# The chunked heads' part of the output projection, by column halves and earlier

## The chip, the cores and the metric

The kernel runs on one core of a Trainium2 chip. The metric is the device time of one execution in microseconds; the time before is the median of three runs. All details come from one profiled execution.

## The reference, cut to what matters

One layer of a streaming encoder, 1024 tokens, 1024 channels, float32. The projection at issue is `mixed`, whose input is the concatenation of two groups of eight heads:

```
q   = rmsnorm(q_lat) @ w_q_up      # latent heads: low-rank q and kv,
kv  = rmsnorm(kv_lat) @ w_kv_up    # "up" projections, rope, QK norm
o_mla = mla_attention(q, k, v)               # 8 heads x 64
o_ca  = chunk_attention(cq, ck, cv, bias)    # 8 heads x 64
mixed = concat([o_mla, o_ca]) @ w_out        # (1024 x 1024) @ (1024 x 1024)
x = x + g_a * mixed
x = x + g_m * gated_conv_mlp(norm(x))
```

Rows 512 to 1023 of `w_out` belong to the chunked heads. Their product needs nothing of the latent heads, so it can be formed while these are still running; the kernel does so and adds the latent heads' share later.

## The kernel before, in words

Every float32 product is made of three matmuls on halves of the numbers: a value is split into a rounded part (`hi_of`, L75, on ScalarE here) and the rest (`lo_of`, L83, mostly on GpSimd), and high x high, high x low and low x high are summed in PSUM (`gemm3`, L150 on; the matmuls are L154, L155 and L156).

The attention runs as 32 units (L974): 16 of the chunked heads and then 16 of the latent heads, each one head and one half of the tokens, with four query tiles of 128 rows. Of each tile `scores` (L735) makes the scores on PE, their minimum on VectorE (L783), the exponential on ScalarE (L790), the scaled probabilities and their rest on GpSimd (L73) and VectorE (L812), and transposes them by a DMA on SyncE's queue (L824). `values` (L829), three tiles later, multiplies by the values on PE (L852), and at the end of a unit the result goes through ScalarE and VectorE (L861, L862) to DRAM, `oT_d`.

All else is given to the attention as filler: `fillers` (L924) is a list of generators in a fixed order, which end with `m` (latent projection), `up0` and `up1` (up projection of latent heads 0 to 3 and 4 to 7, `f_up`, L591) and `oca` (the chunked heads' output projection, `f_oca`, L669). A generator yields the cost in ns of each group of matmuls that it has emitted. `pace` (L961) lets fillers emit as much cost as the attention's own cost times a ratio, `R_CA` = 1.9 in the chunked heads and `R_MLA` = 0.5 in the latent heads (L47). `need` (L952) emits fillers until a named one is done: the first latent unit needs `up0`, the second needs `up1` (L920). Filler groups are tied behind an attention instruction a few steps back (`trail`, L161).

What is emitted is then put in an order for each engine at compile time by a planner that simulates the engines: it takes the ready instruction with the lowest number, where the attention's scores, probabilities and values count as emitted 400, 200 and 200 instructions earlier (L42). On the chip each engine runs its own list in order.

`f_up` emits for each of 8 token tiles nine matmuls (`qu`, `ku`), copies and squares on ScalarE, and norms, rotary and rest on VectorE. `f_oca` loads and splits eight weight tiles (`load_wo`, L657, 128 x 512 each, two column halves), and then for each of 8 token tiles loads 128 x 512 of `oT_d` (`cl`), splits it (`ch`, `cl`), and makes both column halves: 12 matmuls each into a PSUM tile of tag `mm` (two buffers, shared with `f_up`), a copy on ScalarE (`co`, tag `sq`, two buffers) and a store to `part_d`.

Buffers: tag `R` (four) holds the raw rows of `f_up` and `cl`, `ch`; tag `A` (five) holds raw weights; tag `G4` (eight) holds the six split weights of the up projections and then the eight of `f_oca`. After the attention `load_wo(0, n)` (L997) loads the latent heads' eight weight tiles into `G4` again, `o_load` (L1007) the latent results, and the output projection `op` runs on PE.

Of the kernel before, what the change touches and what calls it, by code (L numbers as in the profile page):

```python
# [13 lines left out]
F32 = mybir.dt.float32  # L14
F32R = mybir.dt.float32r
# [49 lines left out]
def layer_kernel(ctx, tc, I, out):  # L65
# [70 lines left out]
    def rtile(name, shape=(P, 512), dt=F32):  # L136
        return apg.tile(list(shape), dt, name=name, tag="R", bufs=4)

    def qtile(name):
        return apg.tile([P, 512], F32, name=name, tag="sq", bufs=2)  # L140
# [450 lines left out]
    def f_up(gr):  # L591
        if gr == 0:
            right.__exit__(None, None, None)
            for i in "4v3":
                G["cm" + i] = tc.tile_pool(name="gp" + i, bufs=1, side="right", reuse_waits="tile")
                G[i] = G["cm" + i].__enter__()
        wq = []
        for k in range(2):
            raw = qtile(f"wqr{gr}_{k}")
            sp.dma_start(raw[:, :384], I["w_qu"][gr][:, k, :])  # L600
            w = g4([P, 2, 512], F32R, f"wq{gr}_{k}")
            hi_of("a", w[:, 0, :384], raw[:, :384])
            lo_of("p", w[:, 1, :384], raw[:, :384], w[:, 0, :384])
            wq.append(w)
        raw = qtile(f"wkr{gr}")
        sp.dma_start(raw[:], I["w_kvu"][gr])
        ssw = cst.tile([P, 1], F32, name=f"sswm{gr}")
        junk = qtile(f"wkj{gr}")
        act.activation(junk[:, 0:256].rearrange("p (a b) -> p a b", a=4),
                       raw[:].rearrange("p (a b) -> p a b", a=4)[:, :, NOPE:], AF.Square, accum_out=ssw[:])  # L610
        vscale["m", gr] = pow2_scale(f"m{gr}", ssw[:], gb2[:], 1, float(KVR))
        sc = vscale["m", gr][0]
        wk = g4([P, 2, 512], F32R, f"wk{gr}")
        hi_of("a", wk[:, 0], raw[:])
        lo_of("p", wk[:, 1], raw[:], wk[:, 0])
        for t in range(NT):
            h, j = divmod(t, 4)
            sl = slice(j * P, (j + 1) * P)
            if t % 2 == 0:
                mq[gr, t // 2] = g3([P, 2, 4, QK], F32, f"qn{gr}_{t}")  # L620
                mk[gr, t // 2] = g3([P, 2, 4, QK], F32, f"kn{gr}_{t}")
                mv[gr, t // 2] = G["v"].tile([P, 2, 4, 2, 64], F16, name=f"vt{gr}_{t}", tag="Gv", bufs=8)
            pt = ps.tile([P, 512], F32, name=f"qu{gr}_{t}", tag="mm", bufs=2)
            yield from gemm3_f(pt[:, :384], [(latT[k, h][:, 0, sl], latT[k, h][:, 1, sl], wq[k][:, 0, :384], wq[k][:, 1, :384])
                                for k in range(2)])
            rq = rtile(f"uqr{gr}_{t}")
            act.activation(rq[:, :384], pt[:, :384], AF.Copy)
            sq = qtile(f"usq{gr}_{t}")
            act.activation(sq[:, :384], rq[:, :384], AF.Square)
            ss = cst.tile([P, 8], F32, name=f"uss{gr}_{t}", tag="ss", bufs=4)  # L630
            r = cst.tile([P, 8], F32, name=f"ur{gr}_{t}", tag="rr", bufs=4)
            dve.tensor_reduce(ss[:, 0:4], sq[:, :384].rearrange("p (a b) -> p a b", a=4), axis=AX.X, op=ADD)
            pt = ps.tile([P, 512], F32, name=f"ku{gr}_{t}", tag="mm", bufs=2)
            yield from gemm3_f(pt[:], [(latT[2, h][:, 0, sl], latT[2, h][:, 1, sl], wk[:, 0], wk[:, 1])])
            p4 = pt[:].rearrange("p (a b) -> p a b", a=4)
            raw = rtile(f"kraw{gr}_{t}")
            r3 = raw[:, :256].rearrange("p (a b) -> p a b", a=4)
            act.activation(r3, p4[:, :, 0:NOPE], AF.Copy)
            s3 = raw[:, 256:512].rearrange("p (a b) -> p a b", a=4)
            act.activation(s3, r3, AF.Square)  # L640
            dve.tensor_reduce(ss[:, 4:8], s3, axis=AX.X, op=ADD)
            dve.tensor_tensor(ss[:, 4:8], ss[:, 4:8], ssr[:, t:t + 1].to_broadcast([P, 4]), op=ADD)
            rsqrt_mean(r[:], ss[:], QK)
            v_t = mv[gr, t // 2][:, t % 2]
            act.activation(v_t[:, :, 0, :], p4[:, :, NOPE:], AF.Copy, scale=sc)
            dve.scalar_tensor_tensor(v_t[:, :, 1, :], p4[:, :, NOPE:], sc, v_t[:, :, 0, :], op0=MUL, op1=SUB)
            q_t = mq[gr, t // 2][:, t % 2]
            dve.tensor_tensor(q_t, rq[:, :384].rearrange("p (a b) -> p a b", a=4),
                              r[:, 0:4].unsqueeze(2).to_broadcast([P, 4, QK]), op=MUL)
            rope_apply(q_t[:, :, NOPE:], q_t[:, :, NOPE:], tabq, t, 4, rq[:, 0:256], dve)  # L650
            k_t = mk[gr, t // 2][:, t % 2]
            dve.tensor_tensor(k_t[:, :, 0:NOPE], r3, r[:, 4:8].unsqueeze(2).to_broadcast([P, 4, NOPE]), op=MUL)
            dve.tensor_tensor(k_t[:, :, NOPE:], kr[:, t:t + 1, :].to_broadcast([P, 4, ROPE]),
                              r[:, 4:8].unsqueeze(2).to_broadcast([P, 4, ROPE]), op=MUL)


    def load_wo(k0, n, he, le):  # L657
        ws = []
        for k in range(k0, k0 + 4):
            raw = atile(f"wor{k}_{n}")  # L660
            sl = slice(n * 512, (n + 1) * 512)
            sp.dma_start(raw[:], I["w_out"][k * P:(k + 1) * P, sl])
            w = g4([P, 2, 512], F32R, f"wo{k}_{n}")
            hi_of(he, w[:, 0], raw[:])
            lo_of(le, w[:, 1], raw[:], w[:, 0])
            ws.append(w)
        return ws

    def f_oca():  # L669
        ws = [load_wo(4, n, "a", "p") for n in range(2)]  # L670
        for t in range(NT):
            lo = rtile(f"cl{t}", (P, 4, P), F32R)
            hi = rtile(f"ch{t}", (P, 4, P), F32R)
            sp.dma_start(f32(lo[:]), oT_d[4:8, :, t * P:(t + 1) * P].rearrange("k p t -> p k t"))
            hi_of("a", hi[:], f32(lo[:]))
            lo_of("p", lo[:], f32(lo[:]), hi[:])
            for n in range(2):
                pt = ps.tile([P, 512], F32, name=f"oc{t}_{n}", tag="mm", bufs=2)
                yield from gemm3_f(pt[:], [(hi[:, k], lo[:, k], ws[n][k][:, 0], ws[n][k][:, 1]) for k in range(4)])
                o = qtile(f"co{t}_{n}")  # L680
                act.activation(o[:], pt[:], AF.Copy)
                sp.dma_start(part_d[t][:, n * 512:(n + 1) * 512], o[:])


    def q2(name):
# [222 lines left out]
    def mla_unit(gr, hh, g):  # L908
        o = hh % 2

        def prep():
# [10 lines left out]
        return u  # L922

    fillers = [("v0", f_v(0)), ("qk1", f_qk(1)), ("qk2", f_qk(2)), ("v1", f_v(1)), ("qk3", f_qk(3)),  # L924
               ("m", f_m()), ("up0", f_up(0)), ("up1", f_up(1)), ("oca", f_oca())]
    done = set()
    side = [f_ada()]
    nside = [0]
# [1 line left out]
    def fill_step():  # L930
        while fillers:
            key, gen = fillers[0]
            try:
                c = next(gen)
            except StopIteration:
                done.add(key)
                fillers.pop(0)
                continue
            if key == "qk1":
                if rope[0] is None:  # L940
                    rope[0] = rope_tables()
                with tc.issue_after(anchor["dve"]):
                    next(rope[0], None)
            if key not in ("v0", "up0", "up1", "oca"):
                nside[0] += c
                while nside[0] > 1700:
                    nside[0] -= 1700
                    next(side[0], None)
            return c
        return None  # L950
# [10 lines left out]
    def pace(cost, ratio):  # L961
        debt[0] += cost * ratio
        while debt[0] > 0:
            c = fill_step()
            if c is None:
                debt[0] = 0.0
                return
            debt[0] -= c

    with tc.issue_after(anchor["pe"]):  # L970
        for _ in range(NPRE):
            fill_step()
# [4 lines left out]
    for n in range(len(tiles) + DEPTH):  # L977
        if n < len(tiles):
            u, i = tiles[n]
            if i % 4 == 0:  # L980
                need(u.need)
                u.prep()
            pace(u.scores(i), R_CA if u.band else R_MLA)
        if n >= DEPTH:
            u, i = tiles[n - DEPTH]
            if i % 4 == 1:
                need(u.needv)
            if i % 2:
                pace(u.values(i), R_CA if u.band else R_MLA)
    need(["oca"])  # L990
    for _ in side[0]:
        pass
# [591 lines left out]
```

## Time and profile before

| What | Value |
|---|---|
| Median of 3 runs (lowest, highest) | 1364.86 us (1364.09, 1369.03) |
| The profiled execution, its span | 1366.2 us, 1364.4 us |
| TensorE clock granted, mean | 0.943 |

Where the time lies, from the profile's table of stretches (busy us of each engine):

| Stretch, us | What runs | PE | DVE | ACT | POOL | Clock |
|---|---|---|---|---|---|---|
| 0 to 98 | norm, modulation, first projection | 68.21 | 72.39 | 43.37 | 52.75 | 0.93 |
| 98 to 393 | chunked heads, projections as filler | 260.44 | 216.69 | 134.56 | 161.85 | 0.90 |
| 393 to 420 | first up projection | 17.95 | 24.18 | 15.81 | 14.29 | 0.92 |
| 420 to 440 | first latent tiles, second up projection begins | 14.78 | 17.22 | 10.57 | 15.90 | 0.60 |
| 640 to 690 | end of attention, output projection | 41.73 | 28.14 | 16.88 | 25.90 | 0.85 |
| 690 to 1364 | gated MLP | 656.89 | 571.21 | 295.96 | 201.03 | 0.99 |

The stretches between 440 and 640, which the change touches, are shown in the prediction. PE is the matmul part of TensorE, PEld its weight loads, DVE is VectorE, ACT ScalarE, POOL GpSimd, SP SyncE, which issues the DMAs. A matmul's busy time overlaps the next one's start, so a busy PE is not one at its peak.

### The profile page before, as it was taken

To read this page: it belongs to the slowest core of one execution; us is meant where nothing else is said; L and a number is where in the kernel's file an instruction comes from. 1 tells how busy PE (TensorE), PEld (TensorE's weight loads), DVE (VectorE), ACT (ScalarE), POOL (GpSimd) and SP (SyncE) were. 2 spreads that over 40 slices of the span, in tenths; PEclk is the share of its full clock that TensorE was granted. 3 is DMA by queue.
4 is the path that set the end of the run, shared out by engine and by line. 5 is a ranking of instruction groups with operands and counts; after the bars stand their busy time and mean duration, and the time that the engine had idled before them with its cause. 6 is when DMAs were issued, how large, how long until landed. Compare 5 with 4: busy or idle time off the path is not lost.

```text
span 1364.4 us, 18704 instructions
## 1 busy us (share of the span) xinstructions
PE 1224.4 (90%) x6168; PEld 1007.3 (74%) x6168; DVE 1103.3 (81%) x1928; ACT 620.9 (46%) x1131; POOL 571.1 (42%) x610
## 2 busy tenths in 40 slices
PE   4889798999877779887898999999999998999998
PEld 3878586877655657665677888888888886888886
DVE  6957879576578997887689888889999997687667
ACT  4443445344455645453357544443344344434331
POOL 5453557376546484334652544443444432000000
PEclk9899797999886879997998999999999999999999
DMA  8413658657222368667940333333333335963441
GB/s 318 136 34 80 144 146 186 166 124 162 62 55 77 72 136 176 143 136 159 374 179 31 112 105 128 104 116 101 131 108 131 104 113 203 369 198 115 125 163 61
DMA packets 223689, 190.57 MB, mean 140 GB/s; under 512 B 148708, under 2 KB 166884, under 8 KB 223592
## 3 DMA queue, kind: packets, MB, share of 16 engines
q1 hardware_dynamic: 223592, 189.38, 48.4%
q8 instruction: 48, 0.79, 0.2%
q14 instruction: 49, 0.40, 0.1%
HBM read 117.24 MB, written 37.49 MB: 113 GB/s over the span
## 4 chain that ended last, share of the span: by engine, by line
PE 31%; DVE 14%; issue 5%; ACT 3%; DMA 3%; POOL 1%; SPq 0%; DVEq 0%; ACTq 0%; POOLq 0%
PE p L1068 4%; PE p L1070 4%; PE p L1069 4%; DVE u L1238 3%; DVE u L1237 2%; PE dnA_P L1395 2%; PE dnA_P L1397 2%; PE dnA_P L1396 2%; PE dnB_P L1395 1%; PE dnB_P L1397 1%; PE dnB_P L1396 1%; ACT u L1236 1%; DVE we L84 1%; DMA PTm<-hlm 1%; DVE ws L1087 1%
## 5 line engine op out<-in xcount | busy, mean ns | idle before, releaser
L77 ACT ACTIVATE dnP<-dnr 128x1024 fp32r<-128x1024 f32 x73 | 77.3, 1062 | 116.4 <-PE dnA_P L1397 46.4
L1369 DVE TENSOR_TENSOR dnP<-dnr,dnP 128x1024 fp32r<-128x1024 f32 x72 | 88.5, 1232 | 51.1 <-ACT dnP L77 51.1
L73 POOL TENSOR_SCALAR hlm<-Pm,rim 128x512 f16<-128x512 f32 (+3 forms) x96 | 67.5, 711 | 76.4 <-ACT Pm L790 21.6
L1237 DVE SCALAR_TENSOR_TENSOR u<-c,cvp,u 128x1023 f32<-128x1023 f32 x44 | 67.1, 1566 | 27.8 <-ACT u L1236 27.8
L84 POOL TENSOR_TENSOR wf<-wu,wf 128x512 fp32r<-128x512 f32 x22 | 38.7, 1757 | 117.6 <-ACT wf L77 117.6
L73 POOL TENSOR_SCALAR hlc<-Pc,ric 128x640 f16<-128x640 f32 (+2 forms) x64 | 47.2, 741 | 71.0 <-DVE ric L793 45.9
L812 DVE SCALAR_TENSOR_TENSOR hlm<-Pm,rim,hlm 128x512 f16<-128x512 f32 (+3 forms) x96 | 67.9, 715 | 9.1 <-POOL hlm L73 8.6
L790 ACT ACTIVATE Pm<-sm,mm 128x128 f32<-128x128 f32 (+3 forms) x64 | 47.2, 738 | 52.7 <-DVE mm L783 32.0
L1236 ACT ACTIVATE u<-c,cvp 128x1024 f32<-128x1024 f32 x44 | 52.3, 1237 | 29.1 <-DVE c L1329 19.1
L852 PE MATMUL pvm<-PTm,vt 128*128 128x256 f16 (+1 forms) x320 | 46.0, 296 | 20.8 <-DMA PTm<-hlm 14.2
L790 ACT ACTIVATE Pc<-sc,mc 128x640 f32<-128x640 f32 (+2 forms) x64 | 42.0, 658 | 48.7 <-DVE mc L779 36.6
L1238 DVE SCALAR_TENSOR_TENSOR u<-c,cvp,u 128x1022 f32<-128x1022 f32 x44 | 63.8, 1488 | 0.0
L812 DVE SCALAR_TENSOR_TENSOR hlc<-Pc,ric,hlc 128x640 f16<-128x640 f32 (+2 forms) x64 | 53.2, 837 | 11.7 <-POOL hlc L73 11.5
L84 POOL TENSOR_TENSOR wb<-wu,wb 128x512 fp32r<-128x512 f32 x22 | 36.4, 1655 | 56.5 <-ACT wb L77 49.5
L852 PEld LDWEIGHTS <-vt 128*128 128x128 f16 x320 | 31.9, 109 | 35.6 <-issue 14.6
L155 PE MATMUL ipq<-wq_s,hT 128*128 128x256 f32 x192 | 55.9, 292 | 0.5 <-POOL wq_s L84 0.5
L154 PE MATMUL ipq<-wq_s,hT 128*128 128x256 f32 x192 | 55.3, 290 | 0.7 <-ACT wq_s L77 0.7
L156 PE MATMUL ipq<-wq_s,hT 128*128 128x256 f32 x192 | 55.4, 289 | 0.0
L77 ACT ACTIVATE wc<-ws 128x512 fp32r<-128x512 f32 x21 | 13.3, 632 | 84.3 <-DVE ws L1087 65.0
L1397 PE MATMUL dnA_P<-dnP 128*128 128x512 f32 x132 | 51.4, 389 | 0.0
L1396 PE MATMUL dnA_P<-dnP 128*128 128x512 f32 x132 | 51.4, 389 | 0.0
L1395 PE MATMUL dnA_P<-dnP 128*128 128x512 f32 x132 | 51.2, 389 | 0.0
(432 smaller groups left out, 4442.3 us busy)
## 6 DMA issues: line engine op xcount, KB each, us to landing
wu<-w_up SPq DMA_DIRECT2D x44, 512.0 KB, 3.5
dnr<-g_d SPq DMA_DIRECT2D x73, 256.0 KB, 2.8
aw<-w_ada SPq DMA_DIRECT2D x48, 256.0 KB, 3.5
g_d<-u SPq DMA_DIRECT2D x22, 512.0 KB, 3.1
dnr<-w_down SPq DMA_DIRECT2D x44, 256.0 KB, 5.4
adaw<-w_ada_a SPq DMA_DIRECT2D x16, 512.0 KB, 5.5
x<-x SPq DMA_DIRECT2D x16, 512.0 KB, 8.8
g_d<-gs SPq DMA_DIRECT2D x22, 256.0 KB, 2.7
```

The source lines that it names most:

```text
L73: pool.tensor_scalar(o, i, s, 1.0, op0=MUL, op1=MUL)
L77: act.activation(o, i, AF.Copy)
L84: (pool if eng == "p" else dve).tensor_tensor(o, i, f32(hi), op=SUB)
L790: act.activation(pr[:, :n], sv, AF.Exp, bias=m[:], scale=-1.0, accum_out=rsum[:, 0:1])
L812: dve.scalar_tensor_tensor(hl[:, w:2 * w], pp, ri[:], hl[:, :w], op0=MUL, op1=SUB)
L852: last = pe.matmul(dst, u.vst(j), mov, start=(x == 0), stop=(x == len(todo) - 1), skip_group_check=True)
L1237: dve.scalar_tensor_tensor(u[:, 1:], c[:, :S - 1], cvp[:, cv + 1:cv + 2], u[:, 1:], op0=MUL, op1=ADD)
L1238: dve.scalar_tensor_tensor(u[:, 2:], c[:, :S - 2], cvp[:, cv:cv + 1], u[:, 2:], op0=MUL, op1=ADD)
L1369: r = f(*a, **k)
L1395: pe.matmul(pt, sh, w[:, 0, 0], start=start, stop=False, skip_group_check=add)
L1396: pe.matmul(pt, sh, w[:, 1, 0], start=False, stop=False, skip_group_check=add)
L1397: pe.matmul(pt, sl, w[:, 0, 0], start=False, stop=stop, skip_group_check=add)
```

## The change

`f_oca` makes one column half for a call, with its own four weight tiles, and loads and splits the eight `oT_d` tiles for that half. A new filler `mix` takes the place of `up1`: it alternates one token tile of the second up projection with one token tile of the first column half. The half's tiles come from tag `A`; `up1` counts as done when its eighth tile is emitted. The filler `oca` then makes the second column half, with tiles of tag `R`, and from the end of `mix` on the pace in the latent heads is 0.6 x 0.5.

```
     def f_up(gr):
         ...
                               r[:, 4:8].unsqueeze(2).to_broadcast([P, 4, ROPE]), op=MUL)
+            yield None

-    def f_oca():
-        ws = [load_wo(4, n, "a", "p") for n in range(2)]
+    def f_oca(n, buf):
+        ws = load_wo(4, n, "a", "p")
         for t in range(NT):
-            lo = rtile(f"cl{t}", (P, 4, P), F32R)
-            hi = rtile(f"ch{t}", (P, 4, P), F32R)
+            lo, hi = (buf(f"c{x}{t}_{n}") for x in "lh")
             sp.dma_start(f32(lo[:]), oT_d[4:8, :, t * P:(t + 1) * P].rearrange("k p t -> p k t"))
             hi_of("a", hi[:], f32(lo[:]))
             lo_of("p", lo[:], f32(lo[:]), hi[:])
-            for n in range(2):
-                pt = ps.tile([P, 512], F32, name=f"oc{t}_{n}", tag="mm", bufs=2)
-                yield from gemm3_f(pt[:], [(hi[:, k], lo[:, k], ws[n][k][:, 0], ws[n][k][:, 1]) for k in range(4)])
-                o = qtile(f"co{t}_{n}")
-                act.activation(o[:], pt[:], AF.Copy)
-                sp.dma_start(part_d[t][:, n * 512:(n + 1) * 512], o[:])
+            pt = ps.tile([P, 512], F32, name=f"oc{t}_{n}", tag="mm", bufs=2)
+            yield from gemm3_f(pt[:], [(hi[:, k], lo[:, k], ws[k][:, 0], ws[k][:, 1]) for k in range(4)])
+            o = qtile(f"co{t}_{n}")
+            act.activation(o[:], pt[:], AF.Copy)
+            sp.dma_start(part_d[t][:, n * 512:(n + 1) * 512], o[:])
+            yield None
+
+    def f_mix():
+        up, oc = f_up(1), f_oca(0, lambda nm: apg.tile([P, 4, P], F32R, name=nm, tag="A", bufs=5))
+        for t in range(NT):
+            for c in up:
+                if c is None:
+                    break
+                yield c
+            if t == NT - 1:
+                done.add("up1")
+            for c in oc:
+                if c is None:
+                    break
+                yield c

-               ("m", f_m()), ("up0", f_up(0)), ("up1", f_up(1)), ("oca", f_oca())]
+               ("m", f_m()), ("up0", f_up(0)), ("mix", f_mix()),
+               ("oca", f_oca(1, lambda nm: rtile(nm, (P, 4, P), F32R)))]

+            if c is None:
+                continue
-            if key not in ("v0", "up0", "up1", "oca"):
+            if key not in ("v0", "up0", "mix", "oca"):

+    def rate(u):
+        return R_CA if u.band else 0.6 * R_MLA if "mix" in done else R_MLA

-            pace(u.scores(i), R_CA if u.band else R_MLA)
+            pace(u.scores(i), rate(u))
-                pace(u.values(i), R_CA if u.band else R_MLA)
+                pace(u.values(i), rate(u))
```

## The prediction

> **What bounds the kernel now.** I read the page first, then busy time by stage, then the stretch that the change touches.
>
> ```profile
> span 1364.4 us, 18704 instructions
> ...
> PE 1224.4 (90%) x6168; PEld 1007.3 (74%) x6168; DVE 1103.3 (81%) x1928; ACT 620.9 (46%) x1131; POOL 571.1 (42%) x610
> ```
>
> The table of stretches has, for each engine, busy us and instructions, then the granted TensorE clock, the DMA share and GB/s:
>
> ```profile
> 440.00:500.00 60.00, 42.27 (x216) 32.82 (x217) 57.18 (x170) 34.29 (x80) 37.89 (x39) 0.83 0.46 96
> 500.00:640.00 140.00, 122.16 (x692) 96.96 (x691) 116.31 (x284) 69.45 (x144) 61.47 (x82) 0.95 0.73 150
> ```
>
> From 440 to 500 us the second up projection runs beside the first latent heads. DVE is the bound: 57.18 of 60 us (95%), while PE is idle for 60 - 42.27 = 17.7 us. From 500 to 640 the rest of the latent attention runs beside the whole chunked-head projection; there PE (87%) and DVE (83%) hinder each other in turn. Where the projection's matmuls (`oc`) lie, and how many softmax tiles pass (one L783 reduction each), is seen in the same table for one tile and for one line:
>
> ```profile
> 500.00:520.00 20.00, 13.51 (x50) 8.90 (x50) 0.00 (x0) 2.37 (x4) 1.00 0.82 155
> 600.00:620.00 20.00, 6.18 (x24) 4.30 (x24) 0.00 (x0) 1.03 (x2) 1.00 0.70 132
> ...
> 480.00:500.00 20.00, 3.11 (x5) 0.66 0.62 138
> 500.00:520.00 20.00, 4.77 (x6) 1.00 0.82 155
> 600.00:620.00 20.00, 5.51 (x9) 1.00 0.70 132
> ```
>
> With 50 projection matmuls in 20 us, 6 tiles pass; with 24 of them, 9 pass; none lies before 500. So the filler is dense where it hurts, and absent where PE waits. The chain of waits over 500 to 640, shares of that window by line, then three of its steps:
>
> ```profile
> by line: DMA PTm<-hlm 8.3%; PE sm L764 7.5%; issue 5.5%; PE pvm L852 5.1%; ACT Pm L790 2.5%; PE oc L154 2.3%; PE oc L155 2.1%; PE oc L156 2.1%; DVE hlm L812 2.0%; ACT om L861 1.5%; POOL hlm L73 1.3%; ACT mk L704 1.0%; DVE mm L783 0.7%; PE m
> ...
> 579.36 0.02 issue
> ...
> 609.66 0.24 PE oc L156
> 609.90 0.23 PE oc L154
> 610.13 0.23 PE oc L155
> ```
>
> The projection holds 2.3 + 2.1 + 2.1 = 6.5% of 140 us, 9.1 us, and all of it behind 579.36, where this chain enters the window. One such matmul costs 0.23 us on the chain (its own duration, about 0.40, overlaps the next).
>
> **The change, part by part.** Instructions that it doubles or moves:
>
> ```profile
> L154 PE MATMUL oc<-wo,ch x64: 392/398/628, 500.7 to 629.9; 128*128 128x512 f32 x64
> ...
> L674 SPq DMA_DIRECT2D cl<-oT_d x8: 377/409/574, 494.3 to 590.4; - x8
> L77 ACT ACTIVATE ch<-cl x8: 622/632/634, 497.6 to 593.5; 128x512 fp32r<-128x512 f32 x8
> L84 POOL TENSOR_TENSOR cl<-cl,ch x8: 1272/1280/1708, 499.6 to 594.2; 128x512 fp32r<-128x512 f32 x8
> ...
> DMA to landing us min/median/max: 3.0/3.2/3.9
> ```
>
> *Matmuls.* Three lines of 64, 192 in all; unchanged. Half, 96 x 0.23 = 22 us of PE time, moves into the stretch of the second up projection.
>
> *Gain in 500 to 640.* By the chain: 9.1 us in the 60.6 us from 579.36 to 640, halved, is 4.55; over 140 us that is 140 / 60.6 x 4.55 = 10.5 us. By the other bound: no DVE work leaves, so 116.31 us at the 95% reached before 500 gives 122 us, a gain of 18 at most. Below, zero: other chains (the transposes' landing) may stand right behind. I take 11, next to the chain row. The later rate, 0.6 x 0.5 = 0.3 of attention cost, spreads the other 96 thinner; by the planner's formulas the remaining attention (L827 and L867 summed: 10.1 us a head, eight heads less the first unit, 78 us) pays for 23 us of filler, and 20.7 are left (96 at 215.8 ns, L172), so the second half should end shortly before the attention does.
>
> *Cost in 440 to 500.* 22 us of matmuls meet 17.7 us of idle PE, so at best 4.4 us stick out. Beside it stands the new split work. Each half now loads and splits its own 8 tiles: 8 more of each row above, 8 x 1.28 = 10.2 us POOL, 8 x 0.63 = 5 us ACT, 8 x 0.41 = 3.3 us on SP's queue and 8 x 256 KB. ACT has 25.7 us idle in the stretch, which hides its part; DMA is 46% busy, which hides the loads if they are issued early. POOL's part touches DVE:
>
> ```profile
> 427.20 2.62 POOL L84 TENSOR_TENSOR wo<-wor,wo 128x512 fp32r<-128x512 f32 x2
> ...
> 427.52 1.17 DVE L462 TENSOR_TENSOR qn<-uqr 128x64 f32<-128x64 f32 x1
> 428.61 1.30 DVE L463 TENSOR_TENSOR qn<-uqr 128x64 f32<-128x64 f32 x1
> ...
> 497.22 0.20 DVE L462 TENSOR_TENSOR qn<-uqr 128x64 f32<-128x64 f32 x1
> 497.34 0.21 DVE L463 TENSOR_TENSOR qn<-uqr 128x64 f32<-128x64 f32 x1
> ```
>
> The same two rotary operations take 0.2 us undisturbed, and 1.17 and 1.30 while POOL runs two splits: about 1 us lost for each. Eight splits enter the stretch, and three weight splits of the other half should leave it:
>
> ```profile
> 477.18 1.35 POOL L84 TENSOR_TENSOR wo<-wor,wo 128x512 fp32r<-128x512 f32 x1
> ...
> 480.11 1.29 POOL L84 TENSOR_TENSOR wo<-wor,wo 128x512 fp32r<-128x512 f32 x1
> ...
> 485.08 1.61 POOL L84 TENSOR_TENSOR wo<-wor,wo 128x512 fp32r<-128x512 f32 x1 [0.92 <-ACT wo L77]
> ```
>
> Net five, 5 us of an engine that is 95% busy. The 4.4 and the 5 lie beside each other, so I take 5, with 0 and 22 (no idle gap usable) as ends. The Trainium skill ("SBUF — State Buffer", section "SBUF: two separate sides") calls the port pair of DVE and GpSimd an exclusive lock: an operation that finds it held waits for the whole instruction. The two rows agree; by that rule alone all eight splits could cost their full 1.28 us, 10 instead of 5, and the net gain would shrink to 3.
>
> *New waits.* In PE's in-order queue the matmuls of each projection tile wait for its load, its ACT copy and its POOL split; scores, values and page transposes queue behind, and DVE waits for those. In SP's queue the load of a tile two ahead waits for a buffer (5 in its pool, two per tile); the probability transposes queue behind it, and the value matmuls wait for them. On ACT the copy out of PSUM waits for PE, with exponentials behind it. All are hidden if the planner's order fits the chip; the price if not is a rival below. The result's copy shares two buffers with the up projection's squares; a buffer is held until its store has landed, a few us against some 7.5 us per up-projection tile (60 us / 8). I cost it at nothing.
>
> *The end.* The last weights (`wo`, second use) now find four of their eight buffers free early:
>
> ```profile
> 642.92 1.54 SPq L662 DMA_DIRECT2D wor<-w_out x3
> 643.54 3.38 PE L852 MATMUL pvm<-PTm,vt 128*128 128x256 f16 x16 [2.77 <-DMA PTm<-hlm]
> ...
> 647.93 0.63 ACT L77 ACTIVATE wo<-wor 128x512 fp32r<-128x512 f32 x1 [1.35 <-DMA wor<-w_out]
> 648.58 0.68 ACT L861 ACTIVATE om<-pvm,vabm 64x512 f32<-64x512 f32 x1
> ...
> 651.21 0.79 PE L154 MATMUL op<-wo,oh 128*128 128x512 f32 x1 [4.29 <-ACT oh L77]
> ```
>
> The last values end at 643.54 + 3.38 = 646.92, but their copy starts only at 648.58, behind a weight copy that waited for its load: 1.7 us. The output projection waits 4.3 us for `oh`, queued behind the same copies. So 1.7 to 4.3 us; I take 2, next to the first, since the next stage hangs on that copy's store.
>
> **Sum:** -11 + 5 - 2 = -8 us. The profiled execution took 1366.2 us (span 1364.4 and 1.8 around it), so 1358.2; it stood 1.3 above the median 1364.86, so 1357 by the median. A measurement here can tell about 0.5%, 6.8 us, so the line lies at 1358.
>
> **Rivals.**
>
> *The gain is taken by the next chain (same).* Landing transposes (8.3%) and issue (5.5%) outweigh the projection's 6.5%. If only 4 of the 11 us remain, -4 + 5 - 2 = -1: 1364. For it: DVE at 83% already. Against: the 9 tiles of 600 to 620.
>
> *POOL is late and PE stands in its queue (slower).* POOL in 480 to 500:
>
> ```profile
> 480.00:490.00 10.00, 4.96 (x21) 3.49 (x20) 9.88 (x25) 6.95 (x17) 8.67 (x10) 0.69 0.39 97
> 490.00:500.00 10.00, 6.64 (x30) 5.16 (x31) 9.97 (x33) 3.73 (x10) 9.74 (x9) 0.62 0.84 180
> ```
>
> POOL is 87 and 97% busy there. A projection tile whose split comes late holds the attention behind it. If all eight tiles wait as long as the L852 row above did for its transposes (2.77 us), 22 us come on top: -11 + 5 - 2 + 22 = +14, 1379. It decides once the wait passes (8 + 6.8) / 8 = 1.9 us per tile. For it: this stretch. Against: in 440 to 480 POOL is much freer.
>
> *Both engines fill up (much faster).* DVE's bound, -18; the up stretch not longer; the end -4: -22, 1343. It needs the granted clock, 0.62 and 0.69 in those rows, to come up as the gaps fill. The Trainium skill ("TensorE: Matmul & The Clock Gate", section "Part 1: The HAM clock gate") says that an idle window of some 3.4 us halves the clock and a busy one restores it. By that rule, steady filler is worth up to 0.17 x 42 = 7 us of PE time in the stretch, an estimate; the rows agree as far as low clocks stand beside idle PE.
>
> *The planner leaves the first half behind the up projection (the change does not do what it says).* Then only the doubled splits stay, 0 to +8, say 1367. Against: in program order each projection tile stands ahead of the next up-projection tile.
>
> **How the numbers follow.** Forecast 0.42 (1350 to 1358); next chain 0.26; POOL late 0.18 (of it, a small part below +14); much faster 0.10; unchanged place 0.04. Faster by over 0.5%: 0.42 + 0.10 = 0.52. Within: 0.26 + 0.04 = 0.30. Slower: 0.18. The range runs from 1344, about the DVE bound, to 1371, where the slower case begins: it leaves out the slower case, and little below.
>
> **What would show it.** Projection matmuls between 440 and 500 and a granted clock above 0.83 there; that stretch about 5 us longer; 8 to 9 tiles per 20 us behind it; POOL's L84 count up by 8 with stretched DVE tensor operations; weight copies for the end before the last values. I am wrong if PE waits on `cl` or `ch` grow from nearly nothing, or if the tile rate behind the up projection stays at 6 to 7.

## The result, and the profile after

The change made the kernel slower by about half a per cent: 1370.87 us (median of 20 runs, 1365.15 to 1376.14) against 1364.47 us for the kernel before (20 runs, 1359.84 to 1369.13), a ratio of 1.0046 with a 95% interval of 1.0030 to 1.0061. That is just inside the 0.5% that the prediction takes as the least a measurement can tell, and on the other side from its forecast of 1357.

The page of the changed kernel, profiled at 1368.91 us, and its table of stretches (columns as in the prediction):

```profile
span 1367.1 us, 18751 instructions
...
PE 1227.5 (90%) x6168; PEld 1010.0 (74%) x6168; DVE 1097.2 (80%) x1928; ACT 625.6 (46%) x1139; POOL 583.7 (43%) x618
```

```profile
440.00:500.00 60.00, 53.27 (x289) 43.39 (x287) 54.57 (x152) 39.95 (x86) 39.27 (x39) 0.97 0.62 150
500.00:640.00 140.00, 114.17 (x622) 88.04 (x622) 118.55 (x304) 70.22 (x150) 67.60 (x86) 0.89 0.75 149
```

The change did what it says: PE fills the early stretch (42.27 to 53.27 us busy) and is thinner behind it (122.16 to 114.17). ACT and POOL have eight instructions more each. The rows of the projection show where:

```profile
L154 PE MATMUL oc<-wo,ch x64: 388/394/793, 431.2 to 618.2; 128*128 128x512 f32 x64
...
L674 SPq DMA_DIRECT2D cl<-oT_d x16: 359/389/542, 346.8 to 587.1; - x16
L77 ACT ACTIVATE ch<-cl x16: 617/632/636, 427.7 to 590.2; 128x512 fp32r<-128x512 f32 x16
L84 POOL TENSOR_TENSOR cl<-cl,ch x16: 1262/1284/2005, 432.8 to 590.9; 128x512 fp32r<-128x512 f32 x16
```

The projection begins at 431.2 instead of 500.7, with 16 loads, copies and splits instead of 8.

A fixed window mixes the early stretch with what follows, so from here the latent attention is cut at events that every version has: its first value matmul, the up projection's last `ku` matmul, and its last value matmul. In the tile view they are the first and last start of these rows; first the kernel before, then the changed one:

```profile
L156 PE MATMUL ku<-wk,latT x16: 390/396/628, 388.8 to 483.7; 128*128 128x512 f32 x16
L852 PE MATMUL pvm<-PTm,vt x320: 218/273/437, 425.7 to 646.6; 128*128 128x256 f16 x128, 128*128 128x128 f16 x32
```

```profile
L156 PE MATMUL ku<-wk,latT x16: 388/396/628, 390.0 to 489.6; 128*128 128x512 f32 x16
L866 PE MATMUL pvm<-PTm,vt x320: 218/273/437, 426.9 to 652.8; 128*128 128x256 f16 x128, 128*128 128x128 f16 x32
```

I call the first part the *up stretch* (58.0 us before, 62.7 after), the second the *rest* (162.9 and 163.2), and the time from the last values to the first activation of the MLP's convolution (its `u`, L1236 before) the *end* (96.6 and 96.2). Busy time in the first two, before and after:

```profile
425.70:483.70 58.00, 43.53 (x221) 34.66 (x221) 52.66 (x153) 33.48 (x76) 34.28 (x37) 0.85 0.37 85
483.70:646.60 162.90, 136.12 (x750) 106.90 (x750) 132.65 (x332) 77.11 (x164) 76.18 (x95) 0.90 0.73 150
```

```profile
426.90:489.60 62.70, 56.62 (x287) 46.11 (x287) 53.47 (x153) 38.86 (x86) 42.05 (x43) 0.93 0.51 122
489.60:652.80 163.20, 125.83 (x686) 96.32 (x685) 133.18 (x335) 78.88 (x166) 80.77 (x98) 0.87 0.77 156
```

In the up stretch the bound has passed from DVE (52.66 of 58.00, 91%) to PE (56.62 of 62.70, 90%), and the stretch is 4.7 us longer. In the rest PE lost 10 us of busy time, yet the rest is not shorter. Softmax tiles (the row reduction, L783 before and L797 after) in the same two parts, before and after:

```profile
410.00:483.70 73.70, 11.81 (x16) 0.81 0.34 79
483.70:650.00 166.30, 35.76 (x48) 0.89 0.74 153
```

```profile
410.00:489.60 79.60, 10.11 (x15) 0.89 0.44 107
489.60:660.00 170.40, 37.39 (x50) 0.86 0.78 165
```

The longer up stretch passes one tile less (16 to 15), which the rest has to make good (49; the second row counts a tile that lies across the cut in both parts). In windows that begin and end at fixed times, near those of the prediction, the same rows are, before and after:

```profile
420.00:500.00 80.00, 13.11 (x18) 0.77 0.42 95
500.00:640.00 140.00, 33.86 (x44) 0.95 0.73 150
```

```profile
420.00:500.00 80.00, 11.07 (x14) 0.88 0.53 127
500.00:640.00 140.00, 35.83 (x48) 0.89 0.75 149
```

Four tiles fewer pass by 500 us, and four more behind it: 44 and 48 tiles in 140 us are 6.3 and 6.9 per 20 us. The chain of waits of the changed kernel, 500 to 640:

```profile
by line: PE sm L778 6.5%; PE pvm L866 5.3%; issue 3.9%; DMA PTm<-hlm 2.4%; ACT Pm L804 2.0%; DVE mm L797 1.9%; DVE hlm L826 1.8%; DVE wo L84 1.4%; DVE mk L719 1.0%; PE oc L154 1.0%; PE oc L156 0.9%; PE oc L155 0.9%; PE mq_ps L706 0.9%; PE m
...
597.43 0.43 PE oc L154
```

The projection's part of this chain fell from 9.1 to 3.9 us. This chain enters the window only at 592.65, so the 3.9 us lie in 47.4 us, where before the 9.1 lay in 60.6: from 15% to 8%, about half, as intended. The time did not follow it.

### The profile page after: what moved, and what is told of

Read it like the earlier page. It is cut to its first block, busy times and chain, and to the rows that moved or that the text cites. A ratio compares the mean times of both kernels' runs of the same rounds, so it can differ in the third digit from the quotient of the medians.

```text
span 1367.1 us, 18751 instructions
## 1 busy us (share of the span) xinstructions
PE 1227.5 (90%) x6168; PEld 1010.0 (74%) x6168; DVE 1097.2 (80%) x1928; ACT 625.6 (46%) x1139; POOL 583.7 (43%) x618
## 4 chain that ended last, share of the span: by engine, by line
PE 29%; DVE 16%; issue 5%; ACT 3%; DMA 2%; POOL 1%; SPq 0%; DVEq 0%; ACTq 0%; POOLq 0%
PE p L1088 3%; PE p L1090 3%; PE p L1089 3%; DVE u L1258 3%; DVE u L1257 3%; PE dnA_P L1415 2%; PE dnA_P L1417 2%; PE dnA_P L1416 2%; PE dnB_P L1417 1%; PE dnB_P L1416 1%; PE dnB_P L1415 1%; ACT u L1256 1%; DVE we L84 1%; DVE ws L1107 1%; DVE c L1349 1%
## 5 line engine op out<-in xcount | busy, mean ns | idle before, releaser
L77 ACT ACTIVATE dnP<-dnr 128x1024 fp32r<-128x1024 f32 x73 | 77.2, 1061 | 116.5 <-PE dnA_P L1417 46.4
L73 POOL TENSOR_SCALAR hlm<-Pm,rim 128x512 f16<-128x512 f32 (+2 forms) x96 | 69.6, 734 | 68.8 <-DVE rim L807 28.1
L1257 DVE SCALAR_TENSOR_TENSOR u<-c,cvp,u 128x1023 f32<-128x1023 f32 x44 | 63.8, 1491 | 27.6 <-ACT u L1256 27.6
L826 DVE SCALAR_TENSOR_TENSOR hlm<-Pm,rim,hlm 128x512 f16<-128x512 f32 (+2 forms) x96 | 65.1, 686 | 6.2 <-POOL hlm L73 5.9
L1258 DVE SCALAR_TENSOR_TENSOR u<-c,cvp,u 128x1022 f32<-128x1022 f32 x44 | 66.9, 1559 | 0.0
L1256 ACT ACTIVATE u<-c,cvp 128x1024 f32<-128x1024 f32 x44 | 52.3, 1238 | 26.1 <-DVE c L1349 16.6
L84 POOL TENSOR_TENSOR wb<-wu,wb 128x512 fp32r<-128x512 f32 x22 | 39.4, 1790 | 57.9 <-ACT wb L77 57.9
L154 PE MATMUL ipq<-wq_s,hT 128*128 128x256 f32 x192 | 56.3, 296 | 1.2 <-ACT wq_s L77 1.2
L155 PE MATMUL ipq<-wq_s,hT 128*128 128x256 f32 x192 | 56.8, 296 | 0.1
L156 PE MATMUL ipq<-wq_s,hT 128*128 128x256 f32 x192 | 56.3, 294 | 0.0
```

The lines of the kernel that those rows point to most:

```text
L73: pool.tensor_scalar(o, i, s, 1.0, op0=MUL, op1=MUL)
L77: act.activation(o, i, AF.Copy)
L84: (pool if eng == "p" else dve).tensor_tensor(o, i, f32(hi), op=SUB)
L826: dve.scalar_tensor_tensor(hl[:, w:2 * w], pp, ri[:], hl[:, :w], op0=MUL, op1=SUB)
L1257: dve.scalar_tensor_tensor(u[:, 1:], c[:, :S - 1], cvp[:, cv + 1:cv + 2], u[:, 1:], op0=MUL, op1=ADD)
L1258: dve.scalar_tensor_tensor(u[:, 2:], c[:, :S - 2], cvp[:, cv:cv + 1], u[:, 2:], op0=MUL, op1=ADD)
```

## The experiments

Every ratio is to the kernel before, run in the same job. Each kernel is one of the two with a small edit; the name in brackets says which.

**First set: the parts of the change.** Is it the thin pace, the alternation, the doubled splits or the matmuls within the up projection?

```
e1_pace    (after)   rate: 0.6 * R_MLA if "mix" in done else R_MLA   ->  R_MLA
e2_halves  (after)   ("mix", f_mix())  ->  ("up1", f_up(1)), ("oc0", f_oca(0, tag A)); rate R_MLA
e3_nosplit (after)   lo_of("p", lo, lo, hi)  ->  only if n; else: lo = hi
e4_fewmm   (after)   for k in range(4)  ->  range(4) if n else range(1)
```

e1_pace:


> The change with the later pace back at 0.5. Compared with the kernel before (ratio 1.0046 for the change). Theory A (the first half's matmuls, twelve in a row in PE's in-order queue, stand ahead of the attention within the second up projection, and about four softmax tiles are lost by 500 us): the pace plays no great part; ratio 1.003 to 1.006, about 14 tiles past the row maximum between 420 and 500 as in the change (18 before). Theory B (the doubled loads and splits, GpSimd's above all, hold VectorE): the same, 1.003 to 1.006. Theory C (the thin pace is at fault, the second half and the last weights come late): most of the loss goes, ratio 0.998 to 1.001.


e2_halves:


> The projection by column halves, with its doubled loads and splits, but both halves behind the second up projection and the pace at 0.5. Theory A: nearly the kernel before, ratio 0.999 to 1.002, and 17 to 18 tiles past the row maximum by 500. Theory B: the doubled work alone makes the loss, 1.003 to 1.006. Theory C: as before, 0.999 to 1.002.


e3_nosplit:


> The change, but the first half leaves out its eight GpSimd splits (its matmuls read the rounded part in place of the rest). Theory A: little changes, ratio 1.002 to 1.005, 14 to 15 tiles by 500. Theory B: the loss goes, ratio 0.997 to 1.000, 17 to 18 tiles by 500. Theory C: as the change, 1.003 to 1.006.


e4_fewmm:


> The change, but the first half makes 3 of its 12 matmuls per token tile (72 of 96 left out, 17 us of PE time), with all of its loads and splits. Theory A: the tiles lost within the up projection come back, 17 to 18 by 500, and the end comes some 10 us sooner than the change, ratio 0.995 to 0.998. Theory B: 14 to 15 tiles by 500, ratio 1.001 to 1.004. Theory C: as B.

Measured: e1 1.0066 (1.0044 to 1.0087), e2 1.0008 (0.9990 to 1.0026), e3 1.0003 (0.9985 to 1.0021), e4 0.9998 (0.9978 to 1.0019). The full later pace does not help, so the thin pace is not the cost. The other three all came back to the level of before, which by total time tells splits and matmuls not apart. The up stretch does. First e3, without the first half's splits, then e4, with 72 of the first half's 96 matmuls left out:

```profile
428.90:491.40 62.50, 57.20 (x286) 47.83 (x286) 51.35 (x156) 38.52 (x87) 30.20 (x36) 0.90 0.52 127
491.40:659.70 168.30, 128.53 (x685) 97.94 (x685) 130.40 (x332) 78.61 (x165) 77.20 (x97) 0.84 0.70 149
```

```profile
427.30:484.20 56.90, 44.37 (x222) 33.35 (x221) 52.38 (x142) 36.90 (x83) 43.77 (x40) 0.91 0.54 129
484.20:654.70 170.50, 128.53 (x679) 98.54 (x678) 139.75 (x346) 80.68 (x170) 83.03 (x101) 0.83 0.74 151
```

Without the splits POOL is 12 us less busy and the up stretch keeps its 62.5 us, PE-bound (57.20). Without the matmuls but with every split it falls to 56.9 us, as long as before, with DVE at 52.38 again. So the matmuls set the length of the up stretch, not the splits. That the splits cost nothing is not shown by this. The expectations went by the softmax tiles that pass between 420 and 500 us: 18 before and 14 in the changed kernel, and 16, 18, 15 and 16 in e1 to e4. Neither leaving out the splits (e3) nor the matmuls (e4) brings all of them back; 17 to 18 were expected of the one that is at fault. In e4's shorter up stretch DVE gets through 142 instructions, where it was 153.

**Second set: what is a matmul worth behind the up projection?**

```
e5_before_fewmm  (before)  gemm of the column halves: for k in (range(1) if n else range(4))
e6_empty         (after)   the edits of e3 and e4 together
e7_loose_before  (before)  u.need = [f"up{gr}"];  R_MLA = 0.7
e8_loose_after   (after)   u.need = [f"up{gr}"];  R_MLA = 0.85
```

e5_before_fewmm:


> The kernel before, but the second column half makes 3 of its 12 matmuls per token tile: 72 matmuls (17 us of PE time) are left out behind 500 us, nothing else is changed. This measures the gain that the prediction expected there (11 us) by itself. Theory D (from 500 us PE is the bound, as the chain of waits seemed to say): ratio 0.990 to 0.994. Theory E (the softmax loop through VectorE, ScalarE and the two score buffers is the bound there, and PE only waits in another place when matmuls go): ratio 0.997 to 1.001, and PE's waits for the exponential grow.


e6_empty:


> The change, but the first half makes 3 of 12 matmuls and leaves out its eight GpSimd splits; loads, ScalarE copies and stores stay. Theory F (splits and matmuls are each a cost within the second up projection, beside one another): 17 to 18 tiles past the row maximum by 500 (14 in the change), ratio 0.993 to 0.998 with theory E, 0.988 to 0.992 with theory D. Theory G (the loss comes from the order alone, the mixed emission, whatever its instructions cost): 14 to 16 tiles, ratio 0.999 to 1.004.


e7_loose_before:


> The kernel before, but the second up projection is needed only by the heads that read it (the fifth latent head), so it is spread over the first four heads at a pace of 0.7. Theory F and E (VectorE is the bound from 420 to 500, since the up projection is emitted at one go): the softmax tiles come more evenly, ratio 0.990 to 0.998. If the total of VectorE's work alone sets the end: 0.998 to 1.002.


e8_loose_after:


> The change, but the mix is needed only by the fifth latent head, paced at 0.85 until it ends and 0.51 after. Theory H (the loss comes from emitting up projection and first half at one go ahead of the second unit, so that they stand before the attention in the queues): ratio 0.992 to 1.000 and 17 or more tiles by 500. Theory F: the splits still hold VectorE and the matmuls still take PE's time, only later: 1.000 to 1.005.

Measured: e5 1.0001 (0.9981 to 1.0022), e6 0.9939 (0.9917 to 0.9960), e7 1.0056 (1.0030 to 1.0082), e8 1.0104 (1.0073 to 1.0135). e7 did not do what it was meant to: its last `ku` matmul starts at 483.2 us, as in before (483.7), so the up projection was not spread. In e8 it was (513.2), and the time rose. e6, with splits and matmuls both gone, is 0.6% faster than before and 1.07% faster than the change, and 18 tiles pass by 500 us, as before: together they do seem to cost something, but a kernel with that much left out is no version to keep. The telling one is e5; its two parts:

```profile
427.00:485.80 58.80, 47.20 (x224) 37.31 (x224) 52.95 (x153) 34.51 (x79) 34.53 (x37) 0.81 0.38 84
485.80:652.90 167.10, 128.22 (x676) 100.03 (x674) 133.66 (x335) 77.87 (x165) 75.84 (x95) 0.83 0.72 154
```

72 of 192 projection matmuls are gone from the rest, which by the forecast's price (10.5 us for 96) is 8 us. The rest takes 167.1 us, against 162.9 in before and 166.4 on the mean of five orders of before (fourth set). What PE waits for between 500 and 640 (total us, times, longest), in before, then in the changed kernel, then in e5:

```profile
PE sm L764 <- ACT Pm L790: 5.8, 6, 2.1
...
PE pvm L852 <- DMA PTm<-hlm: 3.1, 3, 1.8
```

```profile
PE sm L778 <- ACT Pm L804: 13.4, 12, 2.8
PE pvm L866 <- DMA PTm<-hlm: 9.7, 10, 2.5
```

```profile
PE sm L764 <- ACT Pm L790: 14.8, 10, 4.8
PE pvm L852 <- DMA PTm<-hlm: 8.5, 9, 2.2
```

Where the matmuls left, PE waits instead: the score matmuls for the exponential that frees their buffer, the value matmuls for the transposes. Before's 8.9 us of these two waits are the fewest among the five orders of it in the fourth set (8.9 to 20.9, mean 14.9); the changed kernel's five have 18.7 to 24.1, mean 21.4. So the direction holds, at about half the size that the two kernels show.

**Third set: is DVE the bound of the rest, or is it the planner's order?**

```
e9_before_lessdve   (before)  latent heads without the factor 2^15 on ri (64 DVE operations of 0.14 us),
                              made up for in the end scale
e10_before_nosplit  (before)  lo_of("p", lo, lo, hi)  ->  lo = hi  in f_oca
e11_after_lessdve   (after)   the edit of e9
e12_pace055         (before)  R_MLA 0.5 -> 0.55
```

e9_before_lessdve:


> The kernel before, but the latent heads leave out VectorE's scaling of the reciprocal row sum (one of two small operations, 64 x 0.14 us = 9 us of VectorE work and as much in each tile's chain); the factor is taken out of the end scale too, so the result only loses digits. Theory I (from 420 to 640 us VectorE, in the softmax loop, is the bound): ratio 0.990 to 0.997. If the bound is elsewhere: 0.998 to 1.002.


e10_before_nosplit:


> The kernel before, but the eight GpSimd splits of the chunked heads' results are left out (the matmuls read the rounded part for both); they lie behind 500 us there. Within the up projection eight such splits were worth 0.43%. Theory J (a split costs because VectorE's two-input operations of the up projection are held by it; behind 500 there are hardly any such): ratio 0.998 to 1.002. Theory I with GpSimd in the softmax chain: 0.994 to 0.998.


e11_after_lessdve:


> The change with the same VectorE operation left out as in e9. Theory I: it gains as much as e9 gains on the kernel before or a little more (VectorE is the bound there too), so it stays 0.3 to 0.5% above e9. If the loss of the change is VectorE's load alone: it comes level with e9.


e12_pace055:


> A control: the kernel before with the pace in the latent heads at 0.55 in place of 0.5, nothing else. It gives the planner another order of the same work. If the order alone moves the time as much as the change did (theory K), the ratio lies outside 0.997 to 1.003; theories A to J expect 0.998 to 1.002.

Measured: e9 1.0021 (1.0001 to 1.0042), e10 1.0095 (1.0064 to 1.0126), e11 1.0043 (1.0017 to 1.0069), e12 1.0057 (1.0035 to 1.0079). Nine microseconds of DVE work less gain nothing that shows. e11's up stretch is 70.8 us long and its rest 159.0. A kernel with eight POOL splits less is 0.95% slower, and a pace of 0.55 in place of 0.5, with the same work, is 0.57% slower. Each edit lets the planner write another order on all engines, and that alone moves the time by as much as the change did. So a single pair of kernels does not settle differences of half a per cent here.

**Fourth set: siblings.** Both kernels with nothing but the pace shifted, to see the scatter of orders:

```
n_b045, n_b048, n_b052  (before)  R_MLA = 0.45, 0.48, 0.52
n_a050, n_a055, n_a065  (after)   0.6 * R_MLA  ->  0.5, 0.55, 0.65 * R_MLA
```

n_b045:


> The kernel before with the pace at 0.45 (1713 lines of difference on PE). Theory K: 1.002 to 1.009. Theory L: 0.998 to 1.002.


n_b048:


> The kernel before with the pace at 0.48: the same work in another order of each engine (1812 lines of difference on PE). Theory K (the time of the latent stage hangs on which order the planner happens to make, and the kernel before has a good one): the siblings of the kernel before lie above it, 1.002 to 1.009. Theory L (the order hardly matters near the chosen pace, the change's loss is its own): 0.998 to 1.002.


n_b052:


> The kernel before with the pace at 0.52 (1480 lines of difference on PE). Theory K: 1.002 to 1.009. Theory L: 0.998 to 1.002.


n_a050:


> The change with the later factor 0.5 (1300 lines of difference on PE). Theory K: anywhere from 1.000 to 1.010. Theory L: 1.003 to 1.006.


n_a055:


> The change with the later factor 0.55 in place of 0.6 (1208 lines of difference on PE). Theory K: anywhere from 1.000 to 1.010, and on the mean of its siblings no worse than those of the kernel before. Theory L: 1.003 to 1.006, as the change.


n_a065:


> The change with the later factor 0.65 (1282 lines of difference on PE). Theory K: anywhere from 1.000 to 1.010. Theory L: 1.003 to 1.006.

With e12 and e1 there are five orders of each design (e1 is the factor 1.0). Ratios with intervals; the three parts in us, each from one profiled execution:

| Kernel | Ratio to before (95%) | Up stretch | Rest | End |
|---|---|---|---|---|
| before, 0.50 | 1 | 58.0 | 162.9 | 96.6 |
| n_b045 | 1.0029 (1.0004 to 1.0053) | 56.1 | 162.8 | 103.2 |
| n_b048 | 1.0086 (1.0053 to 1.0119) | 56.9 | 171.5 | 102.3 |
| n_b052 | 1.0016 (0.9994 to 1.0037) | 57.5 | 163.7 | 100.4 |
| e12, 0.55 | 1.0057 (1.0035 to 1.0079) | 56.0 | 171.3 | 97.3 |
| **mean of before's orders** | **1.0038** | **56.9** | **166.4** | **100.0** |
| after, 0.6 | 1.0046 (1.0030 to 1.0061) | 62.7 | 163.2 | 96.2 |
| n_a050 | 1.0045 (1.0020 to 1.0071) | 63.0 | 166.2 | 97.7 |
| n_a055 | 1.0071 (1.0046 to 1.0096) | 62.4 | 167.6 | 96.8 |
| n_a065 | 1.0042 (1.0021 to 1.0064) | 61.9 | 163.9 | 96.8 |
| e1, 1.0 | 1.0066 (1.0044 to 1.0087) | 62.5 | 170.7 | 96.7 |
| **mean of after's orders** | **1.0054** | **62.5** | **166.3** | **96.8** |
| e3, no splits in half 1 | 1.0003 (0.9985 to 1.0021) | 62.5 | 168.3 | 93.6 |
| e4, 72 matmuls less in half 1 | 0.9998 (0.9978 to 1.0019) | 56.9 | 170.5 | 95.6 |
| e5, 72 matmuls less behind | 1.0001 (0.9981 to 1.0022) | 58.8 | 167.1 | 96.6 |
| e6, as e3 and e4 | 0.9939 (0.9917 to 0.9960) | 57.9 | 161.5 | 93.1 |

The ratios within a family lie about 0.3% apart (standard deviation over the five before orders), so 0.16% between the family means, 2.2 us, is not told from nothing (standard error about 0.17%). Three of before's four siblings lie within the 1.002 to 1.009 that Theory K expected, n_b052 (1.0016) does not. The kernel before has the best of its five orders. The up stretch is different: its five values lie within 2.0 us and 1.1 us, and the families are 5.6 us apart with a standard error of 0.4. (e11, which also leaves out some of DVE's work, shows that an order can depart from this.) The rest differs by -0.1 (error 2.4) and the end by -3.1 (error 1.3). One of the longer rests, n_b048:

```profile
433.10:490.00 56.90, 44.58 (x217) 34.28 (x217) 52.38 (x155) 33.04 (x76) 34.88 (x37) 0.86 0.39 88
490.00:661.50 171.50, 141.23 (x754) 109.45 (x753) 132.16 (x333) 79.36 (x166) 80.91 (x96) 0.88 0.71 148
```

DVE did the same work there as in before (132.16 against 132.65 us) in 8.6 us more time: the engine's work stayed, the gaps grew.

## Why the prediction was wrong, point by point

**The step that failed: "Gain in 500 to 640 ... I take 11".** The rest was to become 11 us shorter and stayed as long (-0.1 us, error 2.4, between the families; +0.3 between the two kernels). Even credited with the tile that the up stretch no longer passes (163 / 48 = 3.4 us), it gave a third of the forecast. The price came from the chain of one execution: the projection's matmuls stood on it for 9.1 us. I took this as time that goes when they go, and stretched it from the 60.6 us that the chain covers over 140.

Two things speak against it. In the changed kernel their share of the chain did fall by half, without a gain of that size. And e5 leaves 72 of them out, without the rest of the change. Its rest, 167.1 us, lies at the mean of before's orders, 166.4, where the forecast's price wants 158.5; the orders scatter by 4.5 us, so this alone would not rule the price out. But 44 tiles pass between 500 and 640 in e5, as in before, where the price wants 46 to 47 and before's five orders have 43 to 45. The prediction's own sign did not come either: 8 to 9 tiles per 20 us were to pass behind the up projection, 6 to 7 were to show it wrong, and 6.9 passed. That sign did not fit its sum, though: 44 tiles in 129 us, 11 less than 140, are only 6.8. By the fixed windows the gain looks better, as the next point says.

What took the gain's place is seen only as waits: for the exponential and for the transposes. That it would be DVE was not borne out (e9: 9 us less work, rest 166.5 us, one order). The lower clock in the rest (last section) may have taken back a part. Which part of the softmax's loop sets the rest stays open.

The rival "the gain is taken by the next chain" named this, with 4 of the 11 us left and 1364 us. It was right in kind.

**"Cost in 440 to 500", 5 us: the longer stretch was forecast, the lost tile was not.** The up stretch is 5.6 us longer (error 0.4), and one softmax tile fewer passes in it, some 3.4 us to be made up later: 9 us in place of 5. With the fixed windows the account is split otherwise. Over the five orders of each kernel 18.0 and 15.0 tiles pass between 420 and 500 us, and 44.0 and 46.4 between 500 and 640 (error 0.6 in both differences). At 140 / 44 = 3.2 us each, that is a cost of 9.5 us in place of 5, and a gain of 7.6 us in place of 11. Either way both terms were too hopeful; how much of the miss falls on which depends on the cut.

The forecast had two costs that lie beside each other, matmuls that stick out of PE's idle time (4.4 us) and splits that hold DVE (5 us). The length follows the first: e4 takes the matmuls away and the stretch is back to 56.9 us, with all splits in it; e3 takes the splits away and it stays at 62.5. The projection's matmuls in the up stretch of the changed kernel (the table of stretches for tile `oc`):

```profile
426.90:489.60 62.70, 21.51 (x84) 15.38 (x84) 0.00 (x0) 4.08 (x7) 0.93 0.51 122
```

In the up stretch of before PE is idle for 58.00 - 43.53 = 14.5 us; seven tiles of 12 matmuls enter it, 84 x 0.23 = 19.3 us, and 4.8 us stick out. That this is so near the 4.7 us measured is luck in part, since PE still is idle for 62.70 - 56.62 = 6.1 us. Of the 21.5 us, some 8.4 went into idle time, 8.4 into time that other matmuls took before (18 fewer of these, and a higher clock), and 4.7 made the stretch longer. What makes the tile go missing stays open: leaving out the splits (e3, 15 tiles ahead of the cut), the matmuls (e4, 14) or both (e6, 15) does not bring it back by this count, and n_b048, an order of before, passes 15 too.

The splits stretched DVE's operations less than forecast, although six more of them lie in the up stretch (13 in place of 7), where five were reckoned. In the up stretch DVE was busy for 53.47 us instead of 52.66, with 153 instructions both times: 0.8 us where 5 were forecast (52.3 to 52.7 and 53.3 to 54.6 over the five orders). The operation that shows it most is the query's scaling by its norm, between 420 and 505 us (busy us, mean ns), before and after:

```profile
L648 DVE TENSOR_TENSOR qn<-uqr,ur 128x384 f32<-128x384 f32 x9 | 6.1, 675 | 0.5 <-POOL ur L118 0.5
```

```profile
L648 DVE TENSOR_TENSOR qn<-uqr,ur 128x384 f32<-128x384 f32 x9 | 7.9, 878 | 0.7 <-POOL ur L118 0.7
```

With the first half's splits left out (e3) it still takes 800 ns, so not all of this is theirs; and the two rotary operations of the prediction's rows (L462, L463) take 315 and 340 ns on the mean, where it was 385 and 349. DVE is no longer the bound when this happens (53.47 of 62.70 us), so the length of the stretch does not show it. In e4, where DVE is the fullest engine again (52.38 of 56.90), L648 takes 1035 ns. The Trainium skill ("SBUF — State Buffer", section "SBUF: two separate sides") has DVE wait for GpSimd's whole instruction when it finds their common ports held. A mean over nine operations does not show single waits, so these rows neither confirm nor refute it; e3 shows that the length of the stretch did not hang on it.

**"The end", -2 us: the waits went as forecast, the time did not follow.** The last weight copy now comes long before the last values:

```profile
620.49 0.63 ACT L77 ACTIVATE wo<-wor 128x512 fp32r<-128x512 f32 x1
...
653.84 0.68 ACT L875 ACTIVATE om<-pvm,vabm 64x512 f32<-64x512 f32 x1
```

```profile
651.40 1.68 PE L866 MATMUL pvm<-PTm,vt 128*128 128x256 f16 x8 [1.96 <-DMA PTm<-hlm]
652.83 0.78 PE L154 MATMUL op<-wo,oh 128*128 128x512 f32 x1
```

The values end at 651.40 + 1.68 = 653.08 and their copy starts at 653.84, 0.8 us later instead of 1.7, and the output projection starts without the 4.3 us of waiting. Between the two measured kernels only 0.4 us of it shows (96.6 to 96.2), and `op` waits elsewhere instead. Before, it waits on other engines and DMAs 9.6 us for `oh` and 2.8 for `ol`, after 7.3 us for `ol` and 5.3 for a DMA: 12.4 and 12.6 in all. Between the families the end is 3.1 us shorter (error 1.3), but not for the forecast's reason: in three of before's five orders (n_b048, n_b052, e12) the last weight copy starts 12 us or more ahead of the last values, and their ends, 102.3, 100.4 and 97.3 us, are no shorter than before's. That 3.1 lies near 2 is luck as far as these runs show.

**"POOL is late and PE stands in its queue" did not happen.** PE's waits for `cl` or `ch`, which were to grow if it did, are not among its listed waits of the up stretch, where the first half runs, nor of 500 to 640. In the up stretch POOL is busy for 42.05 of 62.70 us. "Both engines fill up" had its condition fulfilled, a granted clock of 0.93 there, and still no gain came of it.

**The base of the sum.** By the families the change is -0.1 + 5.6 - 3.1 = +2.4 us in place of -8, near the 2.2 us between their mean ratios. The spans of the same ten profiled executions differ by -0.3 us (error 4.0), so whether the change as such is slower is not settled; 8 us faster lies far outside what the ratios allow. The two kernels that were compared lie 6.4 us apart. The difference is the order: before stands 0.38% under the mean of its family, 5 us, and the changed kernel 0.08% under that of its own. The prediction priced an edit as if the order of everything else stayed; no run here keeps it.

No version here beat the kernel before with the full computation.

## What to carry to other kernels

A line's share of the chain of waits is the time that it stood last in one execution, not what comes back when it is removed; leave it out once, by itself, before building on its price. Where a planner orders the instructions, compare families of neighbouring parameter values and stages cut at events, since a pace of 0.48 instead of 0.50 moved this kernel by 0.9% with the same work. Filler put into an engine's gaps is not free up to the idle time of that stretch: here 21.5 us of it left 6.1 of 14.5 us idle, took the place of other work and made the stretch 4.7 us longer. A stretch is priced by its length and by the work that passes in it, together.

## What the runs showed of the hardware

The granted TensorE clock rose where the filler went and fell where it left. In the up stretch it rose from 0.85 (0.85 to 0.87 over before's five orders) to 0.93 (0.92 to 0.94), and in the rest it fell from 0.90 (0.88 to 0.91) to 0.87 (0.83 to 0.87). e5, with 72 of the filler's matmuls left out, has 0.83 in its rest. But its up stretch, where nothing was left out, also has a lower clock than before's (0.81), so that fewer matmuls bring the clock down is likely here, not shown. The chain rows from 597.43 on show what it means: six projection matmuls take 0.43 us each there, at a granted clock of 0.50 between 597.4 and 600, where 0.23 was usual. Whether this cost time, or only stands beside PE's waits, the runs do not separate.

Executions of one and the same kernel differ with the mean granted clock: over the changed kernel's 20 runs (1365 to 1376 us) time and clock correlate at -0.84 (in the experiments' kernels from -0.09 to -0.89). A single profiled execution is therefore some microseconds uncertain in its stages, which is why the table above is read by its means.
